# Ten, nine, ten and eight seven-product couples in the down projections, all their sums made ahead

## The chip, the cores and the metric

The kernel runs on one core of one Trainium2 chip. The metric is the device time of one execution in microseconds. A program is run several times, and the median counts. Beside the runs there is one profiled execution, whose trace gives every duration quoted here.

## The reference, cut to what matters

A two-layer encoder trunk: x is 256 tokens by 2048 features, everything in float32. Each layer is norm, token mixer, residual, norm, feed-forward, residual. Layer 0's mixer is a bidirectional mLSTM, layer 1's a bidirectional HGRN2. The change touches the feed-forward, and in it the product with `w_down`:

```
def conv_glu(hn, w_up, conv_w, conv_b, w_down):     # D_FF = 5504
    u = hn @ w_up
    a, v = jnp.split(u, 2, axis=-1)
    ...
    return (jax.nn.gelu(c, approximate=False) * v) @ w_down
```

## The kernel before, in words

**Tiles.** The 5504 hidden features are 43 tiles of 128. They are worked through in two parts: part 0 has 22 tiles, part 1 has 21. For each part there is first an up projection (one chunk per tile: 16 k-tiles, two 128-column halves, gelu and the convolution at its end), then a down stage, which adds the part's share of the down product to the residual `hm`. So a layer has four stretches: up, down, up, down.

**Products in three matmuls.** A float32 operand is split in a high part and a rest (`wh`, `wl` for weights). `parts` (L140) makes them: ScalarE copies the high part, VectorE subtracts it. A product is three matmuls, high x high, high x rest, rest x high, each 128 x 512 here.

**Chunk pairs and couples.** A down stage has two chunk pairs: output columns 0 to 1023, then 1024 to 2047. A pair walks its part's tiles two at a time; such a couple (a unit `u` in the code) is a 2 x 2 block product: two token halves by two column halves, summed over two tiles A11, A12 (tokens of half 0) and A21, A22 (half 1), with the weight blocks B11, B12, B21, B22 of 512 columns each. An ordinary couple takes eight products. A couple in `SEVEN` takes seven, by the Strassen-Winograd scheme: with token sums S1 to S4 (`token_sums`, L561, made at the end of the up chunk of the couple's second tile) and weight sums T1 to T4 (four VectorE subtractions of 128 x 512). The products P1, P5, P6, P7 gather in four PSUM banks of the pool `psm`, C11, C12, C21 in banks of the pool `psa`. After the last seven `mid` (L581) brings the P banks into `hm` (one copy, six VectorE additions, two on GpSimd); after the last couple `done` adds the four C banks. In the very last pair, `ending` (L245) takes over for the last three couples.

**Where the weight sums come from.** Either they are prepared: a generator `prepare` (L613) loads the couple's four blocks (two DMAs of 0.5 MiB), subtracts, and writes the four sums to a DRAM scratch `tscr` (two DMAs); in the down stage `split_squares` (L187) then loads three raw blocks (`raw`), three sums (`T`) and the fourth sum (in the raw tile's last quarter). Or they are made on the fly: `combine` (L202) subtracts inside the down stage, from the raw blocks. `FLY` (L51) lists the couples of each part that are done so: one in three of the four parts, none in layer 1's part 1. The prepared ones are shared out over time: `FIRST` (6) of part 0's first pair before the feed-forward, in the mixer (`prepare_early`, with a period of 25 on the program's clock in layer 0 and 38 in layer 1); the others during the up projections of part 0 and part 1 (`prep`, with a period of the stretch divided by the number of couples). `SPLIT` says how many of part 1's second pair are made in part 0's up projection and how many in part 1's. In the mixers there is a smaller pair of the same kind with three sevens (`SEVEN_MIX`), in layer 0 always on the fly.

**Order.** Side work (sums, norms, heads) sits in generators on a clock that is ticked as matmuls are issued; `until` and `drain` force open work to be issued at once. A planner sets the order of each engine's instructions, apart from those pinned in program order (`pin`, `late`). Weight loads and the writes of sums are issued from SP's queue. Three raw tiles (`RAW`), three `T` tiles shared with the up chunks' scratch (`TEMP`), four plus two pairs of `wh` and `wl` (`WB`, `MORE`; every third piece takes one of the two) go around. A couple's pieces of up to 1024 columns are fetched three ahead (`LOOK`).

## Time and profile before

| What | Value |
|---|---|
| median of 3 runs | 2367.96 us (2366.45 to 2375.84) |
| span of the profiled execution | 2364.5 us |
| PE busy | 2354.1 us |
| DVE busy | 1993.5 us |
| ACT busy | 1470.0 us |
| bytes moved by DMA | 632.97 MB |
| down stages, from the first to the last product | 634 to 742, 975 to 1080, 1909 to 2017, 2250 to 2357 us |

The profile gives no time of the profiled execution apart from its span; what lies around the span is taken as the distance to the median, 3.5 us. PE is TensorE's matmuls, PEld its weight loads, DVE is VectorE, ACT is ScalarE, POOL is GpSimd, SP the queue that starts most DMAs. A duration of a matmul in the trace is its way through the array (390 ns for 512 columns), not the distance to the next; the distance is read from starts.

### The profile page before, as it was taken

The numbers are of one execution on the slowest core, as the hardware profiler recorded it, in microseconds if no ns is written. First come the engines' busy times: TensorE is split into PE (matmuls) and PEld (weight loads), VectorE is DVE, ScalarE is ACT, GpSimd is POOL, SyncE is SP. The second block draws the span as 40 slices with busy tenths as digits, with TensorE's granted clock in tenths as the row PEclk, the third lists the DMA queues.
The fourth block names the chain that finished last, engine by engine and source line by source line (L and its number), as shares of the span: only waits on it lengthen the run. The fifth ranks groups of instructions, "written<-read, shape, count | busy, mean of one in ns | idle before, by whom it ended". The sixth has DMA issues, their size and how long they took to land. (4 is left out here: it accounts for less than half of the span.)

```text
span 2364.5 us, 38407 instructions
## 1 busy us (share of the span) xinstructions
PE 2354.1 (100%) x14545; PEld 2016.2 (85%) x14545; DVE 1993.5 (84%) x3087; ACT 1470.0 (62%) x2340; POOL 196.5 (8%) x244
## 2 busy tenths in 40 slices
PE   9999999999999999999999999999999999999998
PEld 8888888888888888888888888888888888888887
DVE  7777687888998898897888888778789889888888
ACT  7655456555665555676777777776555567455565
POOL 0100000000000000000232322220000000000000
PEclk9999999999999999999999999999999999999999
DMA  8776656888888878996556665646788888888896
GB/s 303 239 248 242 213 195 211 295 282 292 313 321 327 306 282 292 330 334 230 208 203 223 212 225 204 214 169 228 270 300 289 289 321 335 295 287 302 309 351 221
DMA packets 122266, 632.97 MB, mean 268 GB/s; under 512 B 13776, under 2 KB 14928, under 8 KB 77664
## 3 DMA queue, kind: packets, MB, share of 16 engines
q1 hardware_dynamic: 120384, 626.51, 75.0%
q0 software_dynamic: 1120, 3.21, 0.8%
q8 instruction: 114, 1.87, 0.3%
q10 hardware_dynamic: 576, 0.79, 0.1%
q14 instruction: 72, 0.59, 0.1%
HBM read 562.24 MB, written 68.22 MB: 267 GB/s over the span
## 5 line engine op out<-in xcount | busy, mean ns | idle before, releaser
L357 PE MATMUL mm<-xt,wh 128*128 128x512 f32 x3776 | 1312.0, 394 | 0.0
L148 DVE TENSOR_TENSOR wl<-raw,wh 128x1024 fp32r<-128x1024 f32 (+1 forms) x844 | 1037.3, 1234 | 222.6 <-ACT wh L147 214.5
L147 ACT CAST wh<-raw 128x1024 fp32r<-128x1024 f32 (+1 forms) x844 | 875.3, 1042 | 513.0 <-PE mm L357 305.8
L361 PE MATMUL mm<-xt,wl 128*128 128x256 f32 x3776 | 1043.5, 278 | 0.0
L357 PEld LDWEIGHTS mm<-xt,wh 128*128 128x128 f32 x3776 | 705.6, 188 | 160.6 <-issue 0.4
L361 PEld LDWEIGHTS mm<-xt,wl 128*128 128x128 f32 x3776 | 709.4, 188 | 4.5
L373 PE MATMUL mm<-wh,xt 128*128 128x512 f32 x1024 | 324.4, 392 | 0.6 <-ACT wh L147 0.5
L236 PE MATMUL pc<-wh,g 128*128 128x512 f32 (+1 forms) x716 | 243.2, 388 | 0.3 <-ACT wh L147 0.2
L373 PEld LDWEIGHTS mm<-wh,xt 128*128 128x128 f32 x1024 | 191.2, 188 | 40.0 <-ACT wh L147 1.1
L632 DVE TENSOR_TENSOR praw<-praw 128x512 f32<-128x512 f32 x252 | 174.1, 691 | 44.7 <-DMA praw<-in_w_d 29.0
L373 PE MATMUL mm<-wl,xt 128*128 128x512 f32 x512 | 199.7, 391 | 0.0
L236 PEld LDWEIGHTS pc<-wh,g 128*128 128x128 f32 x716 | 134.1, 188 | 29.0 <-ACT wh L147 1.5
L236 PE MATMUL mm<-wh,sx 128*128 128x512 f32 x432 | 153.4, 389 | 0.0
L148 DVE TENSOR_TENSOR wl<-T,wh 128x1024 fp32r<-128x1024 f32 (+1 forms) x144 | 135.9, 955 | 13.3 <-ACT wh L147 8.9
L147 ACT CAST wh<-T 128x1024 fp32r<-128x1024 f32 (+1 forms) x144 | 118.6, 835 | 44.7 <-DMA T<-tscr 18.2
L236 PE MATMUL pc<-wl,g 128*128 128x512 f32 (+1 forms) x358 | 138.8, 388 | 0.0
L591 POOL TENSOR_TENSOR hm<-hm,u 128x512 f32<-128x512 f32 x10 | 14.8, 1481 | 1223.8 <-DVE u L590 1223.8
L373 PEld LDWEIGHTS mm<-wl,xt 128*128 128x128 f32 x512 | 96.2, 188 | 18.6
L1071 DVE TENSOR_TENSOR QK<-QK,G 128x256 f32<-128x256 f32 x224 | 104.6, 515 | 6.2 <-ACT kq L1050 5.9
L1195 ACT COPY avc<-mm 128x256 f32<-128x256 f32 x172 | 64.0, 372 | 63.9 <-PE mm L361 63.6
L1050 ACT COPY kq<-QK 128x512 f32<-128x512 f32 x112 | 74.5, 669 | 37.3 <-DVE QK L1071 29.5
L236 PEld LDWEIGHTS mm<-wh,sx 128*128 128x128 f32 x432 | 81.0, 188 | 16.9 <-ACT wh L147 0.2
(246 smaller groups left out, 2263.1 us busy)
## 6 DMA issues: line engine op xcount, KB each, us to landing
raw<-in_w_up SPq DMA_DIRECT2D x172, 1024.0 KB, 6.1
tscr<-praw SPq DMA_DIRECT2D x126, 512.0 KB, 6.7
praw<-in_w_d SPq DMA_DIRECT2D x120, 512.0 KB, 6.8
raw<-in_w_bq SPq DMA_DIRECT2D x48, 1024.0 KB, 5.0
T<-tscr SPq DMA_DIRECT2D x63, 768.0 KB, 7.6
raw<-in_w_d SPq DMA_DIRECT2D x60, 768.0 KB, 6.0
raw<-in_w_ao SPq DMA_DIRECT2D x24, 1024.0 KB, 4.8
raw<-in_w_d SPq DMA_DIRECT2D x24, 1024.0 KB, 7.7
```

Of the source, the lines that this page charges most:

```text
L147: pin(act.copy(wh[:, :m], r))
L148: pin(dve.tensor_tensor(wl[:, :m], r, wh[:, :m].bitcast(F32), ALU.subtract))
L236: pin(pe.matmul(ps, a, b, start=bank not in begun, stop=stop and i == 2))
L357: hold(pe.matmul(ps[f], wh[:, c:c + P], x, start=k + kk == 0, stop=False))
L361: hold(pe.matmul(ps[f][:, 0:T], wl[:, c:c + P], x[:, 0:T], start=False, stop=k + kk == ch.nk - 1))
L373: pe.matmul(ps[t], x[:, a + t * P:a + (t + 1) * P], w[:, c], start=st and i == 0, stop=sp and i == 2)
L591: pool.tensor_tensor(part(1, 0), part(1, 0), u, ALU.add)
L632: dve.tensor_tensor(out, x, y, ALU.subtract)
L1050: act.copy(m, blocks(QK, h))
L1071: dve.tensor_tensor(two[:, j], two[:, j], by[:, j], ALU.mult)
L1195: act.copy(z, p[:, T:2 * T])
```

## The change

One more couple, couple 0, becomes a seven in each of the four parts, in both of its pairs. Layer 0 has 10 and 9 sevens a pair (it had 9 and 8), layer 1 has 10 and 8 (9 and 7). All their weight sums are prepared; `FLY` is gone. `FIRST` becomes 8, `SPLIT` (0, 4, 5) in layer 0 and (0, 2, 6) in layer 1, and the period of the early sums in layer 1 goes from 38 to 36.

The weights lie in DRAM in the order B12, B11, B22, B21, so that a prepared couple can skip B12 and load B11, B22, B21 in one piece. A seven's pieces come in another order: B21 with T4 (products into C11 and C21), B11 with B22 (C12 and P1), T2 with T3 (P6, P7), T1 (P5). In the second pair of each part couple 0 (`lead`) makes the P products first, then C12, then C11 and C21. The mixers' pairs follow the same new order, with as many sevens as before.

To hold the added token sums, `ones` shrinks to 128 columns, the row `R` of a norm has one buffer instead of two, and `gs` takes the scratch `jk`. The last half's addition in `FinalNorm.half` covers 256 columns, since the bank's other columns hold nothing there.

```diff
-SEVEN = ((1, 2, 3, 4, 5, 6, 7, 8, 9), (1, 2, 3, 4, 5, 6, 7, 8)), ((1, 2, 3, 4, 5, 6, 7, 8, 9), (1, 2, 3, 4, 5, 6, 7))
-FLY = (2,), (5,), (2,), ()
-FIRST = 6
-SPLIT = (0, 2, 5), (0, 2, 5)
+SEVEN = (tuple(range(10)), tuple(range(9))), (tuple(range(10)), tuple(range(8)))
+FIRST = 8
+SPLIT = (0, 4, 5), (0, 2, 6)
...
         def raw(u):
             if u not in raws and u < units:
-                n = 1536 if u in ch.stored else min(2048, 1024 * ch.nk - 2048 * u)
-                raws[u] = load_raw(ch.src, 2048 * u, 2048 * u + n)
+                o = 2048 * u + 512 * (u in ch.stored)
+                raws[u] = load_raw(ch.src, o, min(2048 * (u + 1), 1024 * ch.nk))
                 if u in ch.stored:
                     kept[u] = temporary(ch.pool, "T")
+                    nc.sync.dma_start(raws[u][:, 1536:2048], ch.stored[u][:, 1536:2048])
                     nc.sync.dma_start(kept[u], ch.stored[u][:, 0:1536])
-                    nc.sync.dma_start(raws[u][:, 1536:2048], ch.stored[u][:, 1536:2048])
...
         for u in range(units):
-            r = raw(u)
-            yield *parts(r[:, 0:1024], 1024, more=ch.pool), 1
-            if u + 1 in ch.seven and u + 1 not in ch.stored:
-                combine(u + 1)
+            r, todo = raw(u), []
             if u in ch.seven:
-                yield *parts(kept[u][:, 0:1024], 1024, more=ch.pool), 1
-            if 2 * u + 1 < ch.nk:
-                yield *parts(r[:, 1024:2048], 1024, more=ch.pool), 1
-            if u in ch.seven:
-                yield *parts(kept[u][:, 1024:1536], 512, more=ch.pool), 1
+                T = kept[u]
+                todo = [(r[:, 1024:2048], 1024), (r[:, 0:1024], 1024)] if u in ch.stored else \
+                    [(outer(r), 1024), (r[:, 512:1536], 1024)]
+                todo += [(T[:, 512:1536], 1024), (T[:, 0:512], 512)]
+                if u in ch.lead:
+                    todo.append(todo.pop(0))
+            else:
+                todo = [(r[:, o:o + 1024], 1024) for o in (0, 1024)[:1 + (2 * u + 1 < ch.nk)]]
+            for i, (w, m) in enumerate(todo):
+                yield *parts(w, m, more=ch.pool), 1
+                if i == 0 and u + 1 in ch.seven and u + 1 not in ch.stored:
+                    combine(u + 1)
...
             if u in ch.seven:
                 S1, S3, S2, S4 = ch.sums(u)
-                products((P1, A11, B11), (C12, S4, B22))
-                T2, T3 = piece()
-                products((P6, S2, T2), (P7, S3, T3))
-                B21, T1 = piece()
-                products((C11, A12, B21), (P5, S1, T1))
-                T4, _ = piece()
-                products((C21, A22, T4))
+                lead = u in ch.lead
+
+                def outer(a, b):
+                    T4, B21 = (b, a) if u in ch.stored else (a, b)
+                    products((C11, A12, B21), (C21, A22, T4))
+                if not lead:
+                    outer(a, b)
+                    a, b = piece()
+                    products((C12, S4, b))
+                products((P1, A11, a))
+                products(*zip((P6, P7), (S2, S3), piece()))
+                products((P5, S1, piece()[0]))
                 if u == last:
                     ch.mid(psm_)
                     ch.rest = ch.ends
+                if lead:
+                    products((C12, S4, b))
+                    outer(*piece())
                 continue
...
-            self.R_ = ev.tile([P, T], F32, tag="R", bufs=2, name="R")
+            self.R_ = ev.tile([P, T], F32, tag="R", bufs=1, name="R")
...
             m = 256 if t else 512
+            dve.tensor_tensor(h[:, 0:m], h[:, 0:m], ps[1][:, 0:m], ALU.add)
...
-            prepare_early(mp, 1, 30.0, 38.0)
+            prepare_early(mp, 1, 30.0, 36.0)
...
+                ch.lead = (0,) if c0 else ()
```

50 lines of the change are left out of this document (27 added, 23 removed).

## The prediction

> **What bounds the kernel now.** I read the page's busy times and slices first, then a table of the eight feed-forward stretches, then matmul starts inside one.
>
> ```profile
> span 2364.5 us, 38407 instructions
> PE 2354.1 (100%) x14545; PEld 2016.2 (85%) x14545; DVE 1993.5 (84%) x3087; ACT 1470.0 (62%) x2340; POOL 196.5 (8%) x244
> ...
> GB/s 303 239 248 242 213 195 211 295 282 292 313 321 327 306 282 292 330 334 230 208 203 223 212 225 204 214 169 228 270 300 289 289 321 335 295 287 302 309 351 221
> ```
>
> TensorE is busy in the whole span (and at the full granted clock, 1.00 in the table below), so the time is its count of matmuls times their spacing, plus whatever holes appear. A busy row can hide holes, so spacing has to be read from starts. In the table below the columns are the stretch, its length, then busy time and instructions of PE, PEld, DVE, ACT, POOL, then granted clock, DMA share and GB/s. The rows are: up projection and down stage of part 0 of layer 0, the same of part 1, then layer 1.
>
> ```profile
> 389.00:634.00 245.00, 245.00 (x1419) 214.35 (x1418) 213.31 (x349) 141.02 (x222) 0.70 (x1) 1.00 0.85 294
> 634.00:742.00 108.00, 107.93 (x477) 89.01 (x477) 99.39 (x112) 73.24 (x86) 3.54 (x2) 1.00 0.86 322
> 742.00:975.00 233.00, 233.00 (x1345) 203.75 (x1344) 202.59 (x323) 128.10 (x200) 3.53 (x2) 1.00 0.85 301
> 975.00:1080.00 105.00, 105.00 (x472) 86.98 (x471) 98.12 (x111) 74.72 (x96) 7.01 (x4) 1.00 0.82 299
> 1664.00:1909.00 245.00, 245.00 (x1419) 214.27 (x1418) 210.62 (x345) 139.62 (x221) 0.70 (x1) 1.00 0.84 293
> 1909.00:2017.00 108.00, 107.78 (x477) 88.79 (x476) 102.50 (x116) 72.90 (x88) 3.55 (x2) 1.00 0.88 325
> 2017.00:2250.00 233.00, 233.00 (x1346) 203.75 (x1345) 202.94 (x318) 127.67 (x198) 5.78 (x6) 1.00 0.86 301
> 2250.00:2357.00 107.00, 106.06 (x481) 87.50 (x479) 93.32 (x112) 69.84 (x89) 7.58 (x5) 1.00 0.78 291
> ```
>
> In the second row, 108.00 us over 477 matmuls is 0.226 us a matmul, all but a few of them of 512 columns. VectorE is the second engine: 99.39 of 108 us there, 213.31 of 245 in the stretch before. The 16 DMA engines are the third, at shares of 0.78 to 0.88. Both have room, but both are what the change leans on.
>
> **The change, part by part.**
>
> *Products (the gain).* A couple (two consecutive tiles of 128 features) costs eight products of three matmuls, 24, or seven, 21. Couple 0 of each of four parts becomes a seven in both its chunk pairs: 8 couples, 24 matmuls fewer. 24 x 0.226 = 5.43 us off, if nothing else sets the pace. The Trainium skill, "TensorE: Matmul & The Clock Gate", section "Back-to-back issue gap", gives a sustained roofline of about 131 ns for 512 columns, by which the saving would be an estimated 24 x 0.131 = 3.1 us; the trace does not agree, it has 226 ns.
>
> *Splitting and summing.* These rows group the whole trace by shape (mean ns of one behind the comma):
>
> ```profile
> L148 DVE TENSOR_TENSOR wl<-T,wh 128x1024 fp32r<-128x1024 f32 x72 | 88.3, 1227 | 11.8 <-ACT wh L147 8.4 <-DMA raw<-tscr 3.2
> L148 DVE TENSOR_TENSOR wl<-T,wh 128x512 fp32r<-128x512 f32 x72 | 49.3, 684 | 1.5 <-DMA raw<-tscr 0.9 <-ACT wh L147 0.5
> L632 DVE TENSOR_TENSOR praw<-praw 128x512 f32<-128x512 f32 x252 | 174.1, 691 | 44.7 <-DMA praw<-in_w_d 29.0 <-issue 13.6 <-DMA praw<-in_w_bo 1.4
> L207 DVE TENSOR_TENSOR T<-raw 128x512 f32<-128x512 f32 x18 | 12.4, 686 | 0.8 <-DMA raw<-in_w_d 0.6
> L567 DVE TENSOR_TENSOR avc<-avc 128x128 f32<-128x128 f32 x132 | 38.4, 291 | 3.7
> L569 DVE TENSOR_TENSOR sx<-avc,sx 128x384 fp32r<-128x384 f32 x33 | 18.2, 551 | 0.0
> ```
>
> Each new seven splits 1536 columns more: 1.227 + 0.684 = 1.91 us of VectorE. The six couples summed on the fly (FLY, in both pairs) drop four subtractions each at 0.686. So a down stage of layer 0 part 0 gets 99.39 - 8 x 0.686 + 2 x 1.91 = 97.7 us of VectorE in 108 - 1.36 = 106.6; layer 1's part 0 gets 100.8 in 106.6. Only the last stage, which had no sums on the fly, gets fuller: 93.32 + 3.82 = 97.1 of 105.6. These totals fit.
>
> Prepared couples rise from 63 (252 subtractions over four) to 77: 8 not 6 before the first feed-forward, 11 not 9 in the HGRN, then 16, 14, 14, 14 where 12 stood. Each is 4 x 0.691 = 2.76 us of VectorE, and each part has one more set of token sums, 4 x 0.291 + 0.551 and a short last subtraction, about 2.0. The up projection of layer 0 part 0 becomes 213.31 + 4 x 2.76 + 2.0 = 226.4 of 245 us; the other three 210.1 of 233, 218.1 of 245, 210.5 of 233. Hidden under TensorE as long as 19 us or more stay free, so zero; without that cover 11 us in the first, 5.5 in each other.
>
> *DMA.* A prepared couple reads 1 MiB, writes 1 MiB, and is then read as 0.75 + 0.75 + 0.25 MiB instead of 1. On SP the writes wait for VectorE, and the next raw loads stand behind them. The first up projection goes from 294 to 328 GB/s (4 more couples, 8.4 MB in 245 us). A seven asks for 1.835 MB in 21 x 0.226 = 4.75 us, 386 GB/s, now ten couples on end and not eight. Part 0's down stage asks for 2 x (10 x 1.75 + 1) MiB = 38.8 MB in 106.6 us, 364 GB/s (330 before by the same sum, 322 in the row). Five-us stretches inside today's run of sevens bound what the engines can do (share, GB/s); the first and last of five in a row:
>
> ```profile
> 650.00:655.00 5.00, 1.00 1.00 402
> ...
> 670.00:675.00 5.00, 1.00 1.06 410
> ```
>
> 402 to 410 is above 386, so I count zero; less than that is a rival below.
>
> *The lost cushions (the cost I do count).* An eight costs VectorE two splits for 24 matmuls, a seven nearly four for 21. Starts of the short split of two couples in succession:
>
> ```profile
> 2315.76 0.68 DVE L148 TENSOR_TENSOR wl<-T,wh 128x512 fp32r<-128x512 f32 x1
> ...
> 2319.77 0.68 DVE L148 TENSOR_TENSOR wl<-T,wh 128x512 fp32r<-128x512 f32 x1
> ```
>
> 4.01 us a seven against 4.75 on TensorE: 0.74 is won back per couple. Between the long splits of that run 1.14 us pass, so an eight (2.28 of 24 x 0.226 = 5.42) gives back 3.14. At the change of pairs VectorE also empties eight PSUM banks, 6 + 4 operations at 0.60 from start to start:
>
> ```profile
> 681.98 0.68 DVE L586 TENSOR_TENSOR u<-u,mm 128x512 f32<-128x512 f32 x1
> 682.58 0.68 DVE L587 TENSOR_TENSOR hm<-hm,mm 128x512 f32<-128x512 f32 x1
> ```
>
> 6.0 us. Two eights (the old pair's couple 10, the new pair's couple 0) paid 6.3. Now only one pays, and VectorE falls 2.9 us back on its lead (6.0 - 3.1). The nearest row of such a debt is couple 2 of the second pair, after the four sums on the fly (4 x 0.60 = 2.4) made during couple 1:
>
> ```profile
> 699.59 0.61 PE L236 MATMUL mm<-wh,sx 128*128 128x512 f32 x2
> 700.28 0.50 PE L236 MATMUL pc<-wh,g 128*128 128x512 f32 x1
> 700.62 0.40 PE L236 MATMUL mm<-wh,sx 128*128 128x512 f32 x1
> ```
>
> Two matmuls from 699.59 should bring the next start at 700.04 and then 700.27; they came at 700.28 and 700.62: 0.35 us lost. From below a boundary costs 0 (the lead holds), from above 0.35 + 2.9 - 2.4 = 0.85, if all debt beyond those sums is felt. I take 0.35, four times: 1.4.
>
> *Entering a down stage.* Couple 0 is now consumed at the pace of sevens while the last up chunk's epilogue is still on VectorE. The worst entry now is the last, where VectorE waited for a stored sum and TensorE then for VectorE:
>
> ```profile
> 2252.66 1.23 DVE L148 TENSOR_TENSOR wl<-T,wh 128x1024 fp32r<-128x1024 f32 x1 [3.16 <-DMA raw<-tscr]
> ...
> 2261.79 0.50 PE L236 MATMUL mm<-wl,g 128*128 128x512 f32 x1 [0.53 <-DVE wl L148]
> ```
>
> From below 0, from above a whole 3.2 at each of four entries; near the 0.5 and its like I take 0.25 each, 1.0. Against both stands what the sums on the fly cost now: six at 0 to 0.35, I take 0.2, 1.2 back. Products reordered within a couple, C products last in the second pair's couple 0, T's loads after the shorter ones, the smaller *ones* and *R*: same counts, no queue passed, zero; bounds, a bank waited for or saved once per boundary, lie within those above. The halved last addition (L513) is zero: VectorE stood idle behind it.
>
> ```profile
> 2356.62 0.42 DVE L519 TENSOR_TENSOR hm<-hm,rest 128x256 f32<-128x256 f32 x1 [0.25 <-PE rest L236]
> ```
>
> *Sum.* -5.43 + 1.4 + 1.0 - 1.2 = -4.2 us: span 2360.3. The median of the runs, 2367.96 (2366.45 to 2375.84), is 3.5 above the profiled span; the same distance gives 2363.8.
>
> **The rivals.**
>
> *Given back at the boundaries.* The debt is felt in full above the 2.4: 4 x 0.85 = 3.4 in place of 1.4, and the entries cost 2 in place of 1. Then -5.43 + 3.4 + 2.0 - 1.2 = -1.2, 2366.7. For it: VectorE wins back only 0.74 per couple. Against it: a debt of 2.4 cost only 0.35.
>
> *VectorE held up by the prepared loads (slower).* In the up projections its order is fixed, so a subtraction that waits for its load holds every split behind it:
>
> ```profile
> DVE praw L632 <- DMA praw<-in_w_d: 1.2, 3, 0.6
> ...
> DVE praw L632 <- DMA praw<-in_w_d: 8.9, 4, 3.4
> ```
>
> (layer 0, part 0, then part 1; total, times, longest). In part 0 there are 16 couples and 18.6 us free: it decides from 1.2 us of waiting per couple. With the longest wait, 3.4, for each, 16 x 3.4 - 18.6 = 36 us would be lost; at 1.8, about the double of part 1's 8.9 over twelve, 10.2, and 2.3 and 2.7 in part 1 of the two layers (14 x 1.8 = 25.2 against 22.9 and 22.5). Then 2367.96 - 4.2 + 15.2 = 2379. Against it: 1.2 us in all over twelve couples now.
>
> *DMA as the bound.* If the engines gave over a whole stage only what the best of the page's 40 slices moved, 351 GB/s, and not 402 to 410, part 0's stages would take 38.8 MB / 0.351 = 110.5 us and not 106.6, 7.8 us in the two; part 1's fewer sevens stay under it (36.2 MB, 103.1 of 103.6 us). That gives 2371.6, slower too; it decides from 364 GB/s down. Against it: the 402 to 410, at a share of 1.00 or more. The Trainium skill, "DMA: Bandwidth & Descriptors", section "Where 436 GB/s comes from", says that between HBM and SBUF the HBM side, about 358 GB/s per core, binds; by that rule the two stages would take an estimated 108.4 us each and the time would be 2367.4, but the five-us rows do not agree with it.
>
> *The early sums come too late.* Six couples before the attention's output projection started their subtractions from 96.90 to 255.19:
>
> ```profile
> 96.90 1.42 DVE L632 TENSOR_TENSOR praw<-praw 128x512 f32<-128x512 f32 x2 [1.01 <-DMA praw<-in_w_d]
> ...
> 255.19 1.41 DVE L632 TENSOR_TENSOR praw<-praw 128x512 f32<-128x512 f32 x2
> ```
>
> 31.7 us apart; a seventh and an eighth would start at 287 and 319. But the pool that holds them closes, after all open side work is forced, when that stage's products begin, 322.7 by this row:
>
> ```profile
> L236 PE MATMUL pc<-wh,ya x92: 389/389/389, 322.7 to 364.0; 128*128 128x512 f32 x92
> ```
>
> Load, four subtractions (2.8 us) and store of the last couple would then be issued together. If the next pool's tiles lie over them, I put 5 us in the open: 2369. Against it: the planner may pull a free load forward.
>
> **How the numbers follow.** The forecast has a chance of 0.57 (its own range 2360.5 to 2366.5), boundaries 0.18, early sums 0.08, DMA 0.06, VectorE held up 0.07, something else, that the change doesn't do what it says among it, 0.04. The floor is all 24 matmuls and no new hole, 5.43 plus the 1.2 of the sums on the fly, and a little more from holes at entries: 2360; runs scatter by 1.5 below the median. Range 2358.5 to 2372, which leaves out the upper part of VectorE held up and the rest. A measurement of this kernel tells some 0.5%, 11.8 us, from no change; no sum here gives that much gain, so faster 0.02; slower takes the upper half of VectorE held up and most of the rest, 0.07; within 0.5%, 0.91.
>
> **What would show it.** In the profile after: 24 fewer matmuls in the down stages, sums on the fly in the first attention stage alone, 308 subtractions into *praw*, the four down stages about 1.0 us shorter each (1.36 less the holes), the up projections unchanged at 245 and 233. Wrong would be: an up projection longer by over 1 us with long waits for *praw*; PE waiting for *wl* behind a change of pairs by over 1 us; five-us stretches under 386 GB/s in a run of sevens; a hole near 323.

## The result: 53 us slower, and the profile after

The changed kernel takes 2421.02 us (median of 5 runs, 2419.03 to 2423.82) against 2367.96 us for the kernel before: a ratio of 1.0221 with a 95% interval of 1.0207 to 1.0236. The forecast was 2363.8 us and a range up to 2372.0. The profiled execution has a span of 2419.7 us where the one before had 2364.5, so 55.2 us are to be found in the trace, and 59.4 against the forecast sum of -4.2.

The head of the page after:

```profile
span 2419.7 us, 38584 instructions
PE 2374.2 (98%) x14521; PEld 2016.4 (83%) x14521; DVE 2020.0 (83%) x3159; ACT 1478.8 (61%) x2364; POOL 201.2 (8%) x244
```

The products are as forecast, 14521 matmuls and not 14545. But TensorE, which was busy in 100% of the span, is now at 98%: it is idle for 45.5 us where it was for 10.4. The other 20 us of the loss stand in its busy time, 2374.2 us for fewer matmuls than took 2354.1 before. A busy row hides slower matmuls and short holes. The table of the eight feed-forward stretches (columns as in the prediction: stretch, length, then busy time and instructions of PE, PEld, DVE, ACT, POOL, then granted clock, DMA share, GB/s) says where:

```profile
394.00:639.00 245.00, 245.00 (x1419) 214.27 (x1418) 218.11 (x367) 139.00 (x221) 0.70 (x1) 1.00 0.91 325
639.00:751.00 112.00, 108.55 (x471) 87.12 (x471) 101.11 (x111) 78.59 (x93) 3.87 (x3) 1.00 0.90 337
751.00:988.00 237.00, 234.41 (x1344) 203.75 (x1343) 205.10 (x336) 127.05 (x199) 4.14 (x2) 1.00 0.88 314
988.00:1101.00 113.00, 109.06 (x486) 87.34 (x484) 102.77 (x117) 80.32 (x105) 7.36 (x4) 1.00 0.85 315
1689.00:1946.00 257.00, 251.53 (x1423) 217.34 (x1422) 214.55 (x362) 137.56 (x221) 0.70 (x1) 0.99 0.84 295
1946.00:2057.00 111.00, 107.25 (x467) 86.80 (x466) 100.16 (x109) 78.05 (x93) 3.54 (x2) 1.00 0.88 338
2057.00:2299.00 242.00, 236.36 (x1349) 204.92 (x1348) 204.09 (x330) 125.18 (x197) 6.68 (x6) 1.00 0.87 311
2299.00:2411.00 112.00, 108.09 (x470) 87.31 (x470) 98.63 (x118) 73.63 (x95) 7.55 (x5) 0.97 0.78 291
```

Read the second and the fifth number of each row. In the three up projections that grew (rows 3, 5 and 7), VectorE is busy for 205 of 237, 215 of 257 and 204 of 242 us: it has 32 to 42 us to spare, by its total, and the stage is longer all the same. The down stages (even rows) grew although each has six matmuls fewer (468, 450, 468 and 471 from the first to the last product, against 474, 456, 474 and 477; the rows are cut at whole microseconds and count a few others).

To compare kernels I take the length of each stage from the start of its first main matmul to the start of the next stage's first. In this table (us, worked out from the matmul records of each trace) "order", "counts", "eight", "no wait", "ceiling" and "mended" are experiments of the next section ("mended" is the last one, with 102 warm-up matmuls):

```
stage                before  after  order  counts  eight  no wait  ceiling  mended
mLSTM                 317.1  317.6  317.2   317.5  317.6    317.8    318.3   318.1
its down stage         66.0   70.7   66.0    67.8   70.9     70.6     66.0    66.0
layer 0 part 0 up     245.6  245.6  245.6   245.6  246.2    245.5    245.5   245.6
               down   107.9  111.9  108.2   112.4  112.2    109.3    107.3   107.8
        part 1 up     233.0  237.2  233.0   238.4  236.5    233.0    233.0   233.0
               down   105.8  112.8  105.2   110.9  109.3    106.5    103.8   104.5
HGRN                  515.2  519.6  515.8   521.4  516.3    521.8    522.2   516.8
its down stage         67.6   68.4   67.6    68.7   67.6     68.4     68.4    68.4
layer 1 part 0 up     245.6  256.7  245.5   254.7  245.5    245.5    245.5   245.5
               down   108.1  111.7  109.7   113.4  108.5    108.7    107.1   111.4
        part 1 up     233.0  241.4  233.0   238.2  233.0    233.0    233.0   233.0
               down   114.2  120.8  115.2   120.8  116.9    116.3    113.6   112.8
```

After against before: the up projections +23.7 us, the feed-forward's down stages +21.2, the first attention's down stage +4.7, the HGRN +4.4, the rest about 1.

**What VectorE waits for.** From the waits of the four up projections after, in order of time (total us, times, longest); before they were 1.2, 8.9, 5.2 and 6.7 us:

```profile
DVE praw L649 <- DMA praw<-in_w_d: 8.6, 7, 2.0
...
DVE praw L649 <- DMA praw<-in_w_d: 10.0, 5, 3.7
...
DVE praw L649 <- DMA praw<-in_w_d: 24.6, 10, 4.3
...
DVE praw L649 <- DMA praw<-in_w_d: 17.7, 8, 4.4
```

One of these waits in VectorE's timeline (start, duration, operation; in brackets the idle time before it and what ended it):

```profile
1796.44 0.48 DVE L1218 SCALAR_TENSOR_TENSOR avc<-avc,pp 128x255 f32<-128x255 f32 x1
1801.19 0.69 DVE L649 TENSOR_TENSOR praw<-praw 128x512 f32<-128x512 f32 x1 [4.26 <-DMA praw<-in_w_d]
1801.80 0.48 DVE L1219 SCALAR_TENSOR_TENSOR avc<-avc,pp 128x255 f32<-128x255 f32 x1
1802.19 1.22 DVE L150 TENSOR_TENSOR wl<-raw,wh 128x1024 fp32r<-128x1024 f32 x1
```

The subtraction stands in the middle of an epilogue (L1218, L1219). For 4.26 us VectorE finishes neither that epilogue nor the next split of weights, L150, on which TensorE lives. The load itself was issued at 1789.3 and landed at 1801.1. This wait alone stopped nothing: TensorE's first hole over 0.3 us in that stage comes at 1839.2. The waits use up VectorE's lead over TensorE; then seven holes follow up to 1938.8, the first six about 18 us apart, of 0.46 to 1.97 us from the matmul starts. TensorE's own waits in layer 1's two up projections after (total us, times, longest; before it had none there) say for what:

```profile
PE mm L378 <- DVE wl L150: 5.4, 7, 1.8
...
PE mm L378 <- DVE wl L150: 5.5, 5, 1.9
```

**Entering a down stage.** TensorE's timeline in the last one:

```profile
2304.42 0.81 PE L245 MATMUL pc<-wh,g 128*128 128x512 f32 x2
2305.93 0.80 PE L245 MATMUL pc<-wl,g 128*128 128x512 f32 x1 [0.69 <-DVE wl L150]
2306.52 0.63 PE L245 MATMUL pc<-wh,g 128*128 128x512 f32 x1
2306.95 0.63 PE L245 MATMUL pc<-wl,g 128*128 128x512 f32 x1
...
2310.79 0.63 PE L245 MATMUL mm<-wl,g 128*128 128x512 f32 x1
```

Couple 0 comes at the pace of sevens while VectorE is still late from the up projection. Beside the holes themselves (0.9, 1.0 and 1.0 us within 4.6 us, from start to start less 0.226) the matmuls that follow start 0.43 us apart and not 0.226, with nothing to wait for: the granted clock was 0.50 from 2304.8 to 2311.6, which is why the last row of the table has 0.97.

### The profile page after: what moved, and what is told of

It is laid out like the page before. It is cut to its first block, busy times and chain, and to the rows that moved or that the text cites. A ratio compares the mean times of both kernels' runs of the same rounds, so it can differ in the third digit from the quotient of the medians.

```text
span 2419.7 us, 38584 instructions
## 1 busy us (share of the span) xinstructions
PE 2374.2 (98%) x14521; PEld 2016.4 (83%) x14521; DVE 2020.0 (83%) x3159; ACT 1478.8 (61%) x2364; POOL 201.2 (8%) x244
## 3 DMA queue, kind: packets, MB, share of 16 engines
q8 instruction: 114, 1.87, 0.3%
## 5 line engine op out<-in xcount | busy, mean ns | idle before, releaser
L150 DVE TENSOR_TENSOR wl<-raw,wh 128x1024 fp32r<-128x1024 f32 (+1 forms) x844 | 1032.4, 1232 | 178.1 <-ACT wh L149 169.4
L649 DVE TENSOR_TENSOR praw<-praw 128x512 f32<-128x512 f32 x308 | 212.1, 689 | 95.3 <-DMA praw<-in_w_d 69.0
L245 PE MATMUL pc<-wh,g 128*128 128x512 f32 (+1 forms) x636 | 216.4, 390 | 0.2 <-ACT wh L149 0.2
L245 PE MATMUL mm<-wh,sx 128*128 128x512 f32 x480 | 168.2, 393 | 6.5 <-ACT wh L149 6.4
L150 DVE TENSOR_TENSOR wl<-T,wh 128x1024 fp32r<-128x1024 f32 (+1 forms) x160 | 149.3, 965 | 21.0 <-ACT wh L149 20.9
L149 ACT CAST wh<-T 128x1024 fp32r<-128x1024 f32 (+1 forms) x160 | 129.7, 834 | 55.5 <-DMA T<-tscr 23.4
L245 PEld LDWEIGHTS pc<-wh,g 128*128 128x128 f32 x636 | 119.6, 189 | 26.1 <-ACT wh L149 1.1
L245 PE MATMUL pc<-wl,g 128*128 128x512 f32 (+1 forms) x318 | 124.9, 393 | 5.4 <-DVE wl L150 5.4
L1217 ACT ACTIVATE avc<-avc,pp 128x256 f32<-128x256 f32 x86 | 51.7, 601 | 114.2 <-DVE avc L1215 114.2
L245 PEld LDWEIGHTS mm<-wh,sx 128*128 128x128 f32 x480 | 89.9, 189 | 29.7 <-ACT wh L149 11.3
L390 PEld LDWEIGHTS mm<-wl,xt 128*128 128x128 f32 x512 | 96.4, 188 | 19.2 <-DVE wl L150 0.5
```

Of the source, the lines that this page charges most:

```text
L149: pin(act.copy(h, r))
L150: pin(dve.tensor_tensor(l, r, h.bitcast(F32), ALU.subtract))
L245: pin(pe.matmul(ps, a, b, start=bank not in begun, stop=stop and i == 2))
L390: pe.matmul(ps[t], x[:, a + t * P:a + (t + 1) * P], w[:, c], start=st and i == 0, stop=sp and i == 2)
L649: dve.tensor_tensor(out, x, y, ALU.subtract)
L1217: act.activation(c, a, AF.Identity, bias=col("conv_b", layer * FT + f), scale=cw[1])
```

## The experiments

The edits are shown shortened, as the lines that matter.

**One half of the change at a time.** The change has two halves that can be run apart. The first keeps the counts of before with the new order of pieces and products:

```
-SEVEN = (tuple(range(10)), tuple(range(9))), (tuple(range(10)), tuple(range(8)))
-FIRST = 8
+SEVEN = ((1,...,9), (1,...,8)), ((1,...,9), (1,...,7))
+FLY = (2,), (5,), (2,), ()      # and two() takes fly again
+FIRST = 6                       # SPLIT and the early sums' period as before, too
```

> The new order of a couple's products and pieces, with the counts of before (9, 8, 9 and 7 sevens a pair, couple 0 an eight, six couples summed on the fly, six prepared early, 12 in each up projection). If the counts cost the 53 us (more prepared couples in the up projections, and a down stage entered with a seven), this takes the time of before: 2363 to 2373 us, every stage within 1.5 us of before. If the order costs the down stages' share (the banks of P1, P6, P7 and P5 finish last, so VectorE waits at the change of pairs; a couple summed on the fly needs its sums for its first piece), the up projections stay at 245.6 and 233.0, the four down stages take 15 to 21 us more together and the first attention's down stage 4 to 5 us more: 2387 to 2394 us.

It took 2369.33 us (2368.45 to 2371.21, 10 runs), ratio 1.0008 (0.9999 to 1.0017). The order alone costs nothing that can be told; layer 1's down stages are 1.6 and 1.0 us longer, layer 0's 0.3 longer and 0.6 shorter. (This kernel and the one with couple 0 as an eight keep the halved last addition, and so leave out 256 columns that couple 0 as an eight puts into that bank.)

The second half is the new counts in the old order:

```
 # the kernel before, with
-SEVEN = ((1,...,9), (1,...,8)), ((1,...,9), (1,...,7)); FLY = ...; FIRST = 6; SPLIT = (0, 2, 5), (0, 2, 5)
+SEVEN = (range(10), range(9)), (range(10), range(8));  FIRST = 8; SPLIT = (0, 4, 5), (0, 2, 6)
+# no sums on the fly, the smaller ones and R, the halved last addition
```

> The other half: the new counts (10, 9, 10 and 8 sevens a pair, all sums prepared, early ones every 36 us) with the order of products and pieces of before; the last addition is halved here too. If the counts cost the time, up projections take 20 to 25 us more together and down stages 12 to 20 more, 2400 to 2420 us. If the order costs what the down stages lost, the up projections still take 20 to 25 us more, but the down stages 5 us less than before, and the first attention's down stage stays at 66: 2380 to 2390 us. If what I predicted of the counts were right after all, 2360 to 2372 us.

2420.86 us (2417.22 to 2423.64), ratio 1.0225 (1.0210 to 1.0241): the whole loss. So the cause is in the counts, which I had costed as the gain.

**Couple 0 as an eight, all sums still prepared.**

```
-SEVEN = (tuple(range(10)), tuple(range(9))), (tuple(range(10)), tuple(range(8)))
+SEVEN = (tuple(range(1, 10)), tuple(range(1, 9))), (tuple(range(1, 10)), tuple(range(1, 8)))
-SPLIT = (0, 4, 5), (0, 2, 6)
+SPLIT = (0, 3, 5), (0, 2, 5)
```

> The changed kernel with couple 0 of every pair an eight again (9, 8, 9 and 7 sevens, all prepared ahead, none on the fly; 13, 13, 12 and 12 prepared couples in the up projections where the change has 16, 14, 14 and 14). It has the 24 matmuls of the gain back, 5.4 us. If entering a down stage with a seven costs the down stages' share, they come back to about 108, 106, 108 and 114 us, and if the loss in the up projections goes by the number of prepared couples, those come within 2 us of 245.6 and 233.0: 2368 to 2380 us in all. If the order of products costs the down stages' share, they stay at 110 to 119 us: 2385 to 2400 us.

2387.84 us (2384.56 to 2388.29), ratio 1.0084 (1.0069 to 1.0099), a number inside the second expectation, but not for its reason: the order alone was free in the first run. With 13, 13, 12 and 12 prepared couples the up projections lose 0.6, 3.5, 0 and 0 us: twelve, as before, are free, thirteen no longer (thirteen stand only in layer 0, twelve only in layer 1). The down stages behind an undisturbed up projection (layer 1) are 0.4 and 2.7 us longer than before, behind a disturbed one (layer 0) 4.3 and 3.5. That points to the stage ahead for much of what a down stage loses; the next run tests it.

**The wait taken away.** VectorE's subtractions of the up projections read resident data, so they have no load to wait for; loads and stores go on. The kernel leaves out the sums: what it stores is the weights themselves.

```
             for x, y, out in (...):
+                if ahead:
+                    x, y = hm[:, 0, 0:512], hm[:, 1, 0:512]
+                    out = ev.tile([P, 512], F32, tag="jk", bufs=1, name="jk")
                 dve.tensor_tensor(out, x, y, ALU.subtract)
```

> The changed kernel, in which the prepared couples' subtractions in the up projections read two blocks of the resident residual and write a spare tile; the couples are loaded and stored as before, but what is stored is the weights themselves and not their sums, so the seven-product couples of the feed-forward get wrong sums. VectorE's work, the loads and the stores are all still there; only VectorE's wait for the prepared loads is gone. If that wait is what lengthens the up projections, they return to 245.6, 233.0, 245.6 and 233.0 within 2 us each and the time falls by 18 to 24 us, to 2397 to 2403 us. If VectorE's work or the traffic itself is too much for them, they stay at 245.6, 237, 257 and 241 within 3 us, and the time at 2415 to 2424 us.

2382.50 us (2381.12 to 2383.73), ratio 1.0062 (1.0046 to 1.0079). The same table of this kernel, with part 1 of layer 0 (up projection and down stage) and the up projection of part 1 of layer 1:

```profile
749.00:982.00 233.00, 233.00 (x1346) 203.77 (x1345) 210.28 (x343) 129.51 (x206) 3.62 (x2) 1.00 0.93 327
982.00:1088.00 106.00, 104.04 (x468) 86.00 (x466) 96.74 (x107) 77.22 (x99) 6.47 (x4) 1.00 0.84 317
...
2033.00:2266.00 233.00, 233.00 (x1346) 203.76 (x1345) 208.72 (x336) 128.95 (x204) 5.68 (x6) 1.00 0.93 328
```

All four up projections are back to 245.5 and 233.0 us with TensorE busy throughout, at *more* VectorE work in the stage (210.28 against 205.10) and a higher rate (327 against 314 GB/s). So neither VectorE's fill nor the traffic is too much; the wait is. One thing more goes with it: a store here no longer waits for the subtractions, so buffers come free sooner. This run doesn't part the two; the runs with a queue of their own below keep that order and free part 1's stages all the same. It gave back 38 us of span, more than I expected: 23.9 in the up projections and 16.4 in the four down stages behind them, which VectorE now enters on time, less 2.2 in the HGRN.

**Where the wait comes from: four tries.** My first theory was that SyncE's stores, which wait for VectorE, hold the next loads.

```
-                nc.sync.dma_start(dst[...], loaded[i][j])
+                (nc.gpsimd if ahead else nc.sync).dma_start(dst[...], loaded[i][j])
```

> The changed kernel with one edit: in the up projections the prepared couples' stores are issued by GpSimd and not by SyncE. My theory of the wait: on SyncE a store waits for VectorE's last subtraction, the next raw load stands behind that store and the next prepared load behind the raw load, so a couple costs a whole round (load 9.5 to 10.3 us, subtractions 6, issue 1 to 2: 17.5 us), and 14 rounds fill the 245.6 us of the stage; VectorE, in fixed order, waits in each. By it the prepared loads are issued 5 us or more earlier after the subtractions of the couple before, VectorE's waits for them nearly vanish, the up projections return to 245.6, 233.0, 245.6 and 233.0 within 1.5 us, and the time comes to that of the kernel without the wait, 2380 to 2386 us. Rival: the two buffer sets are the limit (load, subtractions and store of one couple before the next can use them): then the loads come no earlier, and the time stays at 2412 to 2424 us. Second rival: the transfers themselves are slow from the traffic: also 2412 to 2424 us.

2417.77 us, ratio 1.0210 (1.0195 to 1.0225). That theory fell: the loads were issued no earlier relative to VectorE's work (in the median of a stage 0.2 us before to 1.8 us after the last subtraction of the couple before, in the changed kernel 0.2 before to 1.9 after).

The second theory was the place on VectorE: the planner puts the subtractions too close behind their load. Fixing them in written order, first together with the splits, then only against the epilogues' last operation (line 1224):

```
-                dve.tensor_tensor(out, x, y, ALU.subtract)
+                pin(dve.tensor_tensor(out, x, y, ALU.subtract))
 # and, in the first kernel, pin for the up projections' splits; in the second, pin for L1224
```

> The changed kernel with the prepared couples' subtractions and the splits of the up projections' weights kept on VectorE (and the splits on ScalarE) in the order in which they are written, one period behind their load, and not pulled forward by the planner. The stores' queue was not the cause. My theory now: the planner puts a subtraction on VectorE only 7 to 9 us of its work behind the split that frees the raw buffer and so lets SyncE issue the prepared load, and the load takes 9 to 10 us; with 14 or 16 couples VectorE never wins that back. By it the subtractions wait no more, the up projections return to 245.6, 233.0, 245.6 and 233.0 within 1.5 us and the time comes to 2380 to 2388 us. Rival: the distance isn't the cause but VectorE's fill, so that any place in its order is late: up projections as in the changed kernel within 4 us, 2412 to 2425 us; or the fixed order costs more than it brings (splits behind subtractions): over 2425 us.

> The changed kernel with the prepared couples' subtractions kept in written order only against the last operation of each up chunk's epilogue (a dozen of them per stage are anchored in time by TensorE), while the splits stay free. With the splits fixed too, the subtractions stood 16 to 29 us behind their loads and never waited, but the splits lost their lead over TensorE. If the place of the subtractions is the cause, the waits vanish here without that price: up projections 245.6, 233.0, 245.6 and 233.0 within 2 us and 2380 to 2388 us in all. If VectorE has no room for the subtractions wherever they stand, the up projections lose 10 us or more each and the time stays over 2410 us.

2681.18 us, ratio 1.1336 (1.1317 to 1.1356), and 2582.77 us, ratio 1.0909 (1.0893 to 1.0926). The waits for prepared loads did vanish in both, with 12 to 29 us between landing and subtraction (6 to 13 for the last couple of a stage), and the kernels became far slower. The waits of the second one's first up projection show what took their place:

```profile
PEld mm L374 <- ACT wh L149: 37.6, 12, 6.8
ACT wh L149 <- DMA raw<-in_w_up: 36.9, 27, 4.4
```

In the changed kernel this stage has no such wait on ScalarE. Raw loads, prepared loads and the stores of sums are issued by one engine, SyncE, the loads in one written order (the helper at line 412). Its longest kind of wait, first in layer 1's part 0 of the changed kernel, then in the stage of the anchored kernel above:

```profile
SPq L412 <- DVE wl L150: 59.5, 15, 9.6
```

```profile
SPq L652 <- DVE praw L649: 143.7, 23, 17.7
```

In the changed kernel a raw load whose buffer VectorE hasn't freed (L412) holds the prepared load behind it. In the anchored one a store whose subtraction stands late (L652) holds the raw loads behind it; a load waited for a buffer that was still being stored for 15.0 us only. So the first theory's mechanism is there, but not as what costs the changed kernel its time. Delay one side, and the other starves. The same edit with seven early couples and the last seven in the other order:

> The same anchor, seven early couples before the first feed-forward, and the last seven of each pair with its P products first. If the three causes are separate, the up projections are at 245.6 and 233.0, the first attention's down stage at 66.0, the holes at the changes of pairs under 0.4 us: 2368 to 2376 us, still not under the kernel before. If the down stages' entry keeps its losses even with VectorE on time, 2376 to 2384 us.

2595.69 us, ratio 1.0963 (1.0939 to 1.0987); the fully pinned one in that form:

> The same with seven early couples and the last seven of each pair in the other order. If the written order frees the up projections, and the parts add up (4.7 us from the early couples, 3 to 7 from the last seven), 2370 to 2378 us; if it doesn't, 2400 to 2412 us.

2678.54 us, ratio 1.1317 (1.1296 to 1.1338). They stayed with their parents, 13 us over and 3 under.

So the third theory: the shared order couples the two streams. Loads and stores of the up projections' prepared couples both go to GpSimd's queue, without and with the anchor:

```
-  todo, 18.0, (nf * 10.4 - 26.0) / len(todo), finished, late, True))
+  todo, 18.0, (nf * 10.4 - 26.0) / len(todo), finished, nc.gpsimd.dma_start, True))
```

> The changed kernel with both the prepared couples' loads and their stores in the up projections issued by GpSimd, so that neither stands in SyncE's order among the raw loads. If the shared order is what makes the prepared load late (it is issued only when VectorE has freed a raw buffer), the loads are now issued as soon as their own buffer is stored, 8 us or more before they are today, the waits fall to a few us per stage, and the time comes to 2380 to 2390 us. If the planner then pulls the subtractions forward by as much, so that VectorE still stands right behind the load, the waits stay and so does the time: 2408 to 2422 us.

> The same, with the subtractions kept in written order against the epilogue's last operation. The waits are gone (15 us or more between landing and subtraction), and no raw load stands behind a prepared one. If what cost 163 us in the anchored kernel was only the raw loads behind the prepared ones, the up projections are at 245.6 and 233.0 within 2 us and the time is 2380 to 2388 us. If the late subtractions themselves hold VectorE at the wrong moments, the up projections still lose 20 us or more each: over 2450 us.

2398.26 us, ratio 1.0123 (1.0105 to 1.0141), and 2412.04 us, ratio 1.0193 (1.0178 to 1.0208). All subtractions of the program, by shape (total busy, mean ns, then idle time before them and what ended it), in the changed kernel, with only the stores moved, and with the loads moved too:

```profile
L649 DVE TENSOR_TENSOR praw<-praw 128x512 f32<-128x512 f32 x308 | 212.1, 689 | 95.3 <-DMA praw<-in_w_d 69.0 <-issue 22.2 <-DMA raw<-in_w_up 2.5
```

```profile
L649 DVE TENSOR_TENSOR praw<-praw 128x512 f32<-128x512 f32 x308 | 212.7, 691 | 96.7 <-DMA praw<-in_w_d 90.1 <-issue 5.3 <-DMA praw<-in_w_bo 0.8
```

```profile
L649 DVE TENSOR_TENSOR praw<-praw 128x512 f32<-128x512 f32 x308 | 212.7, 693 | 24.4 <-DMA praw<-in_w_d 16.5 <-issue 6.5 <-DMA praw<-in_w_bo 0.8
```

The idle time before the subtractions (what is put down to the load, 69.0 and 90.1, shifts with "issue") stays at 95.3 and 96.7 us and falls to 24.4 only when the loads leave the shared order; both up projections of part 1 are then exactly 233.0. The transfers are hardly faster (median from issue to landing 7.4 us, 8.0 in the changed kernel); they are issued earlier, 6.0 to 9.6 us before the last subtraction of the couple before, in the median of a stage. That shows the coupling, though not its parts: the edit takes the loads off SyncE and out of the fixed order at once. With the anchor all four up projections are at 245.5 and 233.0, although the subtractions stand later: what the anchored kernel lost, it lost on SyncE, by the rows above at the stores. It loses elsewhere: its last couple of the first stage is subtracted at 638.5 to 643.7, when the down stage has begun, and the down stages take 5.9 to 10.0 us more than before. In the kernel without the anchor part 0's up projections are at 254.9 and 252.4, because the planner pulled the now free first loads ahead of the stage (issued from 369.5 on, where the stage begins at 394.3), into the attention's last products and the norm.

**The eighth early couple.** Seven early couples in layer 0, and the stores' queue:

```
-FIRST = 8
+FIRST = 7, 8        # by layer
```

> The edit of the stores' queue, and seven couples instead of eight prepared before the first feed-forward (one more, 17, in the first up projection). If the first attention's down stage lost its 4.7 us because the eighth couple's store held the pool of its token sums until 327, the stage takes 66.0 to 66.5 us again, and the time is 4 to 5 us under that of the stores' edit alone: 2375 to 2382 us. If the new order of pieces costs that stage its 4.7 us, it stays at 70 to 71 us.

The stage takes 66.0 us again, as expected; the whole took 2414.68 us (ratio 1.0200, 1.0183 to 1.0217), 3 us under the stores' queue alone, not the 2375 to 2382 that I wrote on the footing of the first theory. VectorE's timeline shows how the eighth couple did it, first in the changed kernel, then with seven:

```profile
327.33 1.29 DVE L209 TENSOR_TENSOR T<-raw 128x512 f32<-128x512 f32 x2 [1.78 <-DMA tscr<-praw]
328.55 1.42 DVE L690 TENSOR_TENSOR f<-ya 128x256 f32<-128x256 f32 x4
```

```profile
311.18 1.42 DVE L690 TENSOR_TENSOR f<-ya 128x256 f32<-128x256 f32 x4
...
320.91 1.29 DVE L209 TENSOR_TENSOR T<-raw 128x512 f32<-128x512 f32 x2
```

The down stage's pool lies over the one that holds the eighth couple until its store lands at 327.2. Its token sums (L690) start 17 us later, and TensorE then stands for 1.4 and 1.5 us (from the starts) at 335 to 339, with a granted clock of 0.50 from 338.7 to 342.1 behind it.

**The change of pairs.** The last seven multiplied with its P products first, so that its C products run while VectorE empties the P banks (on top of the stores' queue and seven early couples):

```
-                ch.lead = (0,) if c0 else ()
+                ch.lead = (0, max(seven)) if c0 else (max(seven),)
```

> The kernel with seven early couples and the stores' edit, and the last seven of each pair multiplied in the order that couple 0 of the second pair has: its P products first and its C products behind the additions that empty the P banks. If the holes of 1.0 to 1.8 us at the changes of pairs and at the ends of part 0's stages (3.0 and 4.5 us in all in the kernel without the wait) come from VectorE waiting for those banks ahead of its next splits, they shrink to 0.3 us or less each and the time falls by 3 to 7 us against the same kernel without this edit. If they come from VectorE's missing lead, they stay, and so does the time within 1.5 us.

2408.55 us, ratio 1.0175 (1.0160 to 1.0190), 6.1 us under the kernel without it; the holes at the ends of part 0's and part 1's stages (1.17, 0.78 and 1.17 us) fell to under 0.3 us each. In the changed kernel the same place looks so, VectorE and then TensorE:

```profile
742.35 0.69 DVE L602 TENSOR_TENSOR hm<-hm,mm 128x512 f32<-128x512 f32 x1 [2.06 <-ACT u L601]
743.71 0.69 DVE L603 TENSOR_TENSOR u<-u,mm 128x512 f32<-128x512 f32 x1 [0.68 <-PE mm L245]
744.62 0.69 DVE L604 TENSOR_TENSOR hm<-hm,mm 128x512 f32<-128x512 f32 x1 [0.22 <-PE mm L245]
745.22 1.22 DVE L150 TENSOR_TENSOR wl<-raw,wh 128x1024 fp32r<-128x1024 f32 x1
```

```profile
744.42 1.07 PE L245 MATMUL pc<-wh,g 128*128 128x512 f32 x4
746.50 0.50 PE L245 MATMUL pc<-wl,g 128*128 128x512 f32 x1 [1.01 <-DVE wl L150]
```

VectorE follows the P banks one by one as TensorE ends them (2.06 us idle behind ScalarE's copy of the first, then 0.68 and 0.22), and the split for couple 10 stands behind that.

**The old order with these mends.** The new counts, the old order, the stores' queue and seven early couples:

> The new counts in the order of before, with the stores' edit and seven early couples. If only the counts and the wait matter, it takes the same as the same kernel in the new order, within 4 us: 2373 to 2382 us. If the new order is what pays for couples that follow each other without an eight, it takes 5 to 10 us more.

2418.98 us, ratio 1.0219 (1.0204 to 1.0235), 4.3 us over the same kernel in the new order, just past the 4 that I had allowed: the order matters little here too.

**What is left when all three are gone.** The kernel without the wait, with seven early couples and the last seven's P products first; and the own queue with the same two:

> The kernel without the wait (subtractions on resident data, wrong sums stored) with seven early couples and the last seven of each pair with its P products first: the wait, the eighth early couple and the order at the changes of pairs taken away together. If these three are the whole loss, the 5.4 us of the products remain, less about 1 us of entries and the 5 us pause in the HGRN where it appears: 2362 to 2370 us. If entering a down stage with a seven costs by itself, 2372 to 2378 us.

> The own queue without the anchor, with seven early couples and the last seven of each pair with its P products first. 8 to 12 us under the own queue alone: 2370 to 2380 us where that one takes 2380 to 2390, 2398 to 2412 us where it takes 2408 to 2422.

2370.95 us (2369.67 to 2372.12, 10 runs), ratio 1.0011 (1.0002 to 1.0021), and 2384.19 us, ratio 1.0069 (1.0052 to 1.0085). In the first, the eight feed-forward stages sum to 1388.8 us against 1393.2 before: 4.4 us less, where the forecast's sum for them was 4.2. The gain exists. It doesn't show in the time because the HGRN takes 7.0 us more, and the mLSTM and the HGRN's down stage 2.0. The HGRN's TensorE timeline in the changed kernel has the larger part of the reason:

```profile
1396.84 0.84 PE L1075 MATMUL pd<-kq 128*32 128x32 f32 x75
1400.56 0.32 PE L1075 MATMUL pd<-kq 128*32 128x32 f32 x3 [2.88 <-issue]
```

In a run of 32-column matmuls TensorE stands for 2.9 us and waits for nothing that the profile shows ("issue"). Thirteen of the sixteen kernels with 14521 matmuls have this pause, among the last few matmuls of that run, whether they reach it at 1376 or at 1550 us; no kernel with other counts has it.

**The mended kernels.** The own queue with seven early couples and the last seven's P products first, and with the first two couples' loads of each stage left in SyncE's order; and the same with 102 warm-up matmuls in place of 90, to shift that place:

```
-                    start(r[j], ...)
+                    (late if i < 2 else start)(r[j], ...)
-    for i in range(90):
+    for i in range(102):          # second kernel alone
```

> The prepared couples of the up projections on GpSimd's queue, but the loads of the first two of each stage in SyncE's order as in the changed kernel; seven early couples; the last seven of each pair with its P products first. If the free early loads are what lengthened part 0's up projections to 248 and 252 us, all four are at 245.6 and 233.0 within 1 us and the time is 2368 to 2376 us, close to the kernel without the wait (2371.0). If the free loads are not the cause, it stays at 2380 to 2386 us.

> The same with 102 warm-up matmuls in place of 90 (12 small ones at the start, no work changed). If the pause in the HGRN goes with the place in TensorE's instruction stream, it is gone, the HGRN takes 515 to 518 us and the time is 4 to 6 us lower: 2363 to 2371 us, the same as the kernel before or a little under it. If the pause has to do with the time or the traffic there, it stays and so does the time within 1.5 us.

2376.14 us (2373.41 to 2378.49), ratio 1.0033 (1.0021 to 1.0046): part 0's up projections are at 245.6 and 245.5, part 1 of layer 1 still at 238.4 with 18.9 us of waits. And 2371.05 us (2368.82 to 2375.44, 11 runs), ratio 1.0017 (1.0008 to 1.0026). The run of small matmuls in the second one, where the 75 and 3 had the pause between them:

```profile
1378.02 0.87 PE L1075 MATMUL pd<-kq 128*32 128x32 f32 x78
```

The pause is gone and the HGRN is 5.5 us shorter (522.3 to 516.8). In these two profiles layer 1's part 1 differs by another 5.4 us (238.4, 233.0), with no edit there; the first profile is of an execution of 2378.49 us, the longest of its five, and the medians differ by 5.1. No version here beats the kernel before.

The traces show what goes with the pause. Part 3 of the page after lists a DMA queue for instructions (packets, MB, share of 16 engines):

```profile
q8 instruction: 114, 1.87, 0.3%
```

1.87 MB is 64 bytes for each of 14521 matmuls and as many weight loads, so this is most likely TensorE's. In all thirteen kernels a transfer of 16 KB on it starts 0.4 to 1.0 us into the pause (in the changed kernel at 1398.13, in a pause from 1397.68 to 1400.56), and the one before it 17 to 19 us earlier. In the seven kernels without the pause, three with the same number of matmuls among them, one starts 7 to 11 us ahead of that place, and none in it. So TensorE most likely waits there for its instructions. Why the transfer comes late in some kernels isn't shown; the 12 matmuls (24 in the trace) shift the stream against it.

## Why the prediction was wrong, point by point

- **Products, -5.43: right.** 24 matmuls fewer, and 4.4 us in the feed-forward stages once the other causes are away.
- **Prepared sums in the up projections, "hidden under TensorE as long as 19 us or more stay free, so zero": the step that failed.** 23.7 us were lost in the stages. Taking the wait away gave them back with 16.4 of what their successors lost, less 2.2 in the HGRN: 38 of the 55 us. VectorE's total had room (27 to 42 us were free after the change), but a total isn't a reserve: in a fixed order the free time lies behind the wait, and the split that TensorE needs stands there too. By my rule (waits against free time) layer 1's part 0 with 24.6 us of waits against 26.9 free (the forecast's 218.1 of 245) should have lost nothing; it lost 11.1.
- **The rival "VectorE held up by the prepared loads"** named the mechanism and the row to look at, and got 0.07. Its price of 15 us was too low by the same rule, and because it let the delay end with the stage. Of "against it: 1.2 us in all over twelve couples", the other three rows said otherwise: 8.9, 5.2 and 6.7 us of waits at twelve couples were a loop already at its edge. I quoted the 8.9 and argued from the 1.2.
- **Moved DMAs, "the next raw loads stand behind them", zero.** The right sentence, with no price. The issuing order ties raw loads, prepared loads and stores together in both directions; I looked at bandwidth alone.
- **Bandwidth: right.** The changed kernel's runs of sevens moved 408 to 419 GB/s in 5-us stretches from 662 to 677 (the 299 to 355 before that are the entry, where TensorE waited for VectorE), and the ceiling kernel's first down stage took 107.3 us, so the DMA rival's 110.5 us is out. Its row has 349 GB/s and not the 362 of my sum: some of the 38.8 MB is loaded before the stage begins. The Trainium skill's rule that I weighed ("DMA: Bandwidth & Descriptors", section "Where 436 GB/s comes from", about 358 GB/s) would have made it an estimated 108.4. The measured stage is under that, but by its 349 GB/s it doesn't test the rule; the 5-us stretches (378 to 423 GB/s in the ceiling kernel from 650 to 680) don't agree with it.
- **Entering a down stage, 1.0 us: at most 0.3 where VectorE comes on time.** The holes in the first 30 us of the four stages (those over 80 ns, from the matmul starts) add up to 1.6 us before, 1.6 without the wait and 1.9 in the ceiling kernel. In the changed kernel they are 19.2: the term had no cover for a late VectorE.
- **Change of pairs, 1.4 us, and "products reordered ... zero": mis-sized together.** Holes from 40 us on to the last product of the four stages: 0.7 us before, 7.8 without the wait, 1.1 with the last seven's P products first as well. The bound that I put (a bank waited for once per boundary) was there, but at the ends of the second pairs too and not only between the pairs, and up to 1.8 us at one of them.
- **Sums on the fly, 1.2 us back: not measured by itself.** "Order" and "eight" both have couple 0 as an eight and layer 1 undisturbed: part 0's down stage is 1.2 us shorter without the sums (109.7, 108.5), but part 1's, which has none in either, is 1.7 longer (115.2, 116.9), so the pair can't tell.
- **The early sums too late: happened as written**, pools overlapping and token sums waiting, 4.7 us where I had put 5, at a chance of 0.08. The row that I quoted against me (a couple each 31.7 us, the last at 319, the pool needed from 311 on) decided it; "the planner may pull a load forward" was hope.
- **The HGRN's pause** was in no term: the HGRN took 4.4 us more than before, and 5.5 us went with the pause between the two mended kernels.

By controlled removal, in spans: 37.9 us the wait, 12.6 us the eighth early couple and the change of pairs. With about 5.5 us for the pause, taken from the mended pair, an estimate is left of 2363.7 against the 2360.3 of the sum.

## What to carry to other kernels

Before you count work on an engine as hidden by its free time, ask whether anything in it waits, and what stands behind that wait in the engine's order: a prefetch loop whose waits are already some us at today's density will not take a sixth more. Streams of loads and stores in one issuing order wait for each other's buffers, so the stream that feeds the bound engine needs an order of its own.

## What was not expected of the hardware

- **Short holes halve the clock.** After 0.9, 1.0 and 1.0 us of idle TensorE within 4.6 us, the matmuls at 2306 to 2311 started 0.43 us apart and not 0.226, and after the HGRN's 2.97 us pause (in the kernel without the wait) seven in a row at 0.43, some 3 us of them. So these holes cost half as much again as they are long, to nearly twice as much. In the changed kernel the granted clock is 0.50 from 338.7, 1400.3 and 1939.6 for 3.4 us each and from 2304.8 for 6.8, some 17 us in all ahead of the end, or at most 8.5 us of the loss; before, it is nowhere ahead of the end. A hole's length alone doesn't decide: one of 1.97 us at 1938.8 was followed by it, one of 2.10 at 2272.0 wasn't. The Trainium skill, "TensorE: Matmul & The Clock Gate", section "HAM oscillation — how this bites in real kernels", has the rule that no idle gap should pass about 3.4 us. These runs show the drop with no single gap that long.
- **A pause of TensorE tied to a place in the program**, 2.7 to 3.1 us in a run of small matmuls, which 12 small matmuls at the start of the kernel removed. A transfer on the instruction queue goes with it in all thirteen kernels; that TensorE waits for it is likely, not proved.
